# Cross-entropy backward on one core: loading two-row blocks as single transfers, and the last row in two column halves

## The chip, the cores and the metric

The kernel runs on one core of one Trainium2 chip. The metric is the device time of one execution in microseconds (us). The profile's span is 1.7 to 2.0 us shorter than the time of the same execution.

Some words that recur: HBM is the memory outside the core in which input and output lie. SBUF is the core's own memory, in 128 partitions. DMA engines, 16 of them here, copy between the two; loads and stores are issued on two separate DMA queues. VectorE and ScalarE are compute engines of the core. A "packet" is one entry of the profile's record of DMA work; here each packet of data moves one contiguous run of bytes.

## The reference

The input is 8192 rows of 8192 logits in float32 and one label per row. The output is the softmax of each row, with 1 subtracted at the label:

```python
logits_max = np.max(logits, axis=-1, keepdims=True)
exp_logits = np.exp(logits - logits_max)
softmax = exp_logits / np.sum(exp_logits, axis=-1, keepdims=True)
...
return (softmax - one_hot).astype(np.float32)
```

Every byte is read once and written once: 268.4 MB in and 268.4 MB out.

## The kernel before

A "row" of the program is 128 rows of the matrix, one on each SBUF partition, 4 MB (4096 KB) in all. There are T = 64 of them. A block is two neighbouring rows of the program, and in HBM the two lie side by side for each partition: partition p of a block has 2 x 32 KB in one run. SBUF holds six such rows ("slots"), and a row is worked on in place in its slot.

```python
SLOTS = 6
...
x_b = x_nv.rearrange("(b p j) v -> b p j v", p=P, j=G)      # G = 2 rows to a block
X = const.tile([P, SLOTS, V], fp32)
...
def load(t, n):
    free = [stored[u - SLOTS] for u in range(t, t + n) if u - SLOTS in stored]
    w = run(nc.sync, free, got[t % SLOTS], "dma_start", out=sbuf(t, n), in_=hbm(x_b, t, n))
    loaded.update(dict.fromkeys(range(t, t + n), w))

def store(t, n):
    w = run(nc.scalar, [finished[t + n - 1]], put[t % SLOTS], "dma_start", ...)
    stored.update(dict.fromkeys(range(t, t + n), w))
...
for t in range(T):
    # ScalarE: exp with accumulated sum; VectorE: reciprocal
    if t + 1 < T:
        load(t + 1, 1)
        row_max(t + 1)          # VectorE, waits for the load
    if t > 0:
        store(t - 1, 1)
    # ScalarE: scale by 1/sum; VectorE: subtract the one-hot
```

A load waits until the row six earlier has been stored, because it takes that row's slot. And on VectorE the maximum of row t + 1 stands ahead of the one-hot pass of row t, so row t can't be stored before row t + 1 has been loaded.

## Time and profile before

The time is 1248.08 us, the median of 3 runs (1248.03 to 1248.10). What matters of the profile:

| Quantity | Value | View |
|---|---|---|
| DMA engines, share of time busy | 1.00 in the middle | windows |
| Rate moved | 433 GB/s in the middle | windows |
| VectorE | 90% of the span | page, part 1 |
| ScalarE | 74% of the span | page, part 1 |
| One load, issue to landing | 24.2 us (median) | page, part 6 |
| One store, issue to landing | 55.1 us (median) | page, part 6 |

These are lines of the page of the kernel before. The first two are the busy tenths and the rate in 40 slices of the span. Then come the DMA queues (q1 is the loads', q10 the stores'; packets, MB, share of the engines), two groups of VectorE instructions, and the issues (count, KB each, us from issue to landing).

```profile
DMA  9999999999999999999999999999999999999998
GB/s 406 418 430 433 435 434 430 433 435 433 431 434 434 433 431 434 434 432 431 434 435 432 431 434 434 431 433 434 435 431 433 433 434 432 432 433 435 431 432 385
...
q1 hardware_dynamic: 9216, 268.44, 50.0%
q10 hardware_dynamic: 9264, 268.51, 49.9%
...
L64 DVE TENSOR_REDUCE m<-X 128x1 f32<-128x8192 f32 x64 | 555.6, 8681 | 91.4 <-DMA X<-in_logits_dram 91.4
...
X<-in_logits_dram SPq DMA_DIRECT2D x64, 4096.0 KB, 24.2
out_dram<-X ACTq DMA_DIRECT2D x64, 4096.0 KB, 55.1
```

The DMA engines are busy all the time and share themselves equally between loads and stores. VectorE waits 91.4 us in all for loads, about 2 us a row. Stores take long to land because they stand in a queue. With a row of 8.39 MB (in and out) every 19.36 us, the engines set the pace.

The windows view of the kernel before shows the start, the middle and the end. Its columns are the stretch, its length, the busy time of five engines (PE, PEld, DVE, ACT, POOL, with counts), the clock, the DMA share, and GB/s.

```profile
60.00:240.00 180.00, 0.00 (x0) 0.00 (x0) 180.00 (x33) 148.42 (x33) 0.00 (x0) 1.00 1.00 433
400.00:860.00 460.00, 0.00 (x0) 0.00 (x0) 413.34 (x73) 339.46 (x73) 0.00 (x0) 1.00 1.00 433
...
1224.00:1232.00 8.00, 0.00 (x0) 0.00 (x0) 5.57 (x2) 0.26 (x1) 0.00 (x0) 1.00 1.01 434
1232.00:1240.00 8.00, 0.00 (x0) 0.00 (x0) 0.00 (x0) 0.00 (x0) 0.00 (x0) 1.00 1.02 442
```

While the compute engines end their work at about 1230 us, stores are still queued, and the DMA engines stay full until about 1242 us.

The timeline of the kernel before shows when the last two rows arrive, and when the last store is issued (start, length, engine, what, and the idle time before it).

```profile
1179.83 8.69 DVE L64 TENSOR_REDUCE m<-X 128x1 f32<-128x8192 f32 x1 [1.92 <-DMA X<-in_logits_dram]
...
1199.19 8.69 DVE L64 TENSOR_REDUCE m<-X 128x1 f32<-128x8192 f32 x1 [1.94 <-DMA X<-in_logits_dram]
...
1229.60 0.34 ACTq L64 DMA_DIRECT2D out_dram<-X  x1
```

Both maxima start the moment their row has landed. The last row (63) lands 19.36 us after row 62, which is 4.19 MB at 217 GB/s, half of the 433.

### The profile page before, as it was taken

The page shows a single profiled execution, that of the slowest core. Times are in us where ns is not written, and L with a number is a line of the kernel's source. Part 1 is how long each engine was busy: PE and PEld are TensorE (multiplying, and loading weights), DVE is VectorE, ACT ScalarE, POOL GpSimd, SP SyncE. Part 2 cuts the span into 40 slices and gives each one's busy share as a digit, 9 for nine tenths or more (in the row PEclk, how much of TensorE's full clock was granted, in tenths as well). Part 3 has the DMA queues.
Part 4 walks back from the last instruction along what each step waited for, and adds up shares of the span by engine and source line. Part 5 has one row for each costly group of instructions (what it writes and reads, how often), then busy time and mean ns, then how long its engine had stood idle before and what let it go on. Part 6 is the DMA issues. An engine that isn't in the chain of part 4 may idle for free.

```text
span 1246.4 us, 592 instructions
## 1 busy us (share of the span) xinstructions
PE 0.4 (0%) x2; PEld 0.3 (0%) x2; DVE 1121.3 (90%) x196; ACT 919.0 (74%) x194; POOL 7.4 (1%) x7
## 2 busy tenths in 40 slices
PE   0000000000000000000000000000000000000000
PEld 0000000000000000000000000000000000000000
DVE  5999999999988989889898898998988989889893
ACT  3888888888767777677767777777777777677772
POOL 2000000000000000000000000000000000000000
DMA  9999999999999999999999999999999999999998
GB/s 406 418 430 433 435 434 430 433 435 433 431 434 434 433 431 434 434 432 431 434 435 432 431 434 434 431 433 434 435 431 433 433 434 432 432 433 435 431 432 385
DMA packets 18484, 536.98 MB, mean 431 GB/s; under 512 B 2064, under 2 KB 2064, under 8 KB 2096
## 3 DMA queue, kind: packets, MB, share of 16 engines
q1 hardware_dynamic: 9216, 268.44, 50.0%
q10 hardware_dynamic: 9264, 268.51, 49.9%
q14 instruction: 4, 0.03, 0.0%
HBM read 268.50 MB, written 268.44 MB: 431 GB/s over the span
## 4 chain that ended last, share of the span: by engine, by line
another core or an unknown queue 69%; DVE 21%; DMA 6%; SPq 1%; ACT 1%; DVEq 0%; issue 0%; PE 0%; ACTq 0%
DVE m L64 10%; DVE X L64 10%; DMA out_dram<-X 4%; DMA X<-in_logits_dram 2%; SPq L64 1%; ACT X L64 1%; DVE iota L64 0%; DVEq L52 0%; DMA lab_raw<-in_labels_dram 0%; DVE lab_f L64 0%; DVE r L64 0%; PE iota L64 0%; ACTq L64 0%; DVE lab L64 0%
## 5 line engine op out<-in xcount | busy, mean ns | idle before, releaser
L64 DVE TENSOR_REDUCE m<-X 128x1 f32<-128x8192 f32 x64 | 555.6, 8681 | 91.4 <-DMA X<-in_logits_dram 91.4
L64 ACT ACTIVATE X<-X,m 128x8192 f32<-128x8192 f32 x64 | 455.8, 7122 | 187.9 <-DVE m L64 187.9
L64 DVE SCALAR_TENSOR_TENSOR X<-iota,lab,X 128x8192 f32<-128x8192 int16 (+1 forms) x65 | 559.6, 8610 | 4.1 <-ACT X L64 4.1
L64 ACT ACTIVATE X<-X,r 128x8192 f32<-128x8192 f32 (+1 forms) x65 | 456.0, 7016 | 116.0 <-DVE r L64 116.0
L64 DVE RECIPROCAL r<-s 128x1 f32<-128x1 f32 x64 | 9.8, 153 | 7.3 <-ACT X L64 7.3
L64 ACT ACTIVATION_READ_ACCUMULATOR X<-X,m 128x1 f32 x64 | 11.9, 186 | 0.0
L64 DVE CAST lab_f<-lab_raw 32x256 f32<-32x256 int32 x1 | 3.5, 3526 | 4.9 <-DMA lab_raw<-in_labels_dram 4.9
L64 POOL IOTA X<- 128x8192 int16 x1 | 6.9, 6943 | 0.0
L64 DVE TENSOR_SCALAR iota<-X 128x4096 int32<-128x4096 int32 x1 | 4.4, 4427 | 0.1
L64 ACT ACT_TABLE_LOAD x1 | 1.3, 1283 | 1.4 <-SPq L52 1.4
L64 DVE COPY lab<-iota 128x64 f32<-128x64 f32 x1 | 0.2, 224 | 0.5 <-PE iota L64 0.5
L64 PE MATMUL iota<-ident,lab_f 32*128 32x32 f32 x2 | 0.4, 300 | 8.5 <-DVE lab_f L64 8.5
L64 PEld LDWEIGHTS iota<-ident,lab_f 32*128 32x128 f32 x2 | 0.3, 196 | 8.4 <-DVE lab_f L64 8.4
L64 POOL TENSOR_SCALAR_AFFINE_SELECT ident<-ident 32x32 f32<-32x32 f32 x1 | 0.2, 202 | 0.1
L64 POOL MEMSET ident<- 32x32 f32 x1 | 0.1, 114 | 0.5 <-SPq L52 0.5
L176 POOL MEMSET const-bfloat16-1.0<- 128x1 bf16 x1 | 0.1, 106 | 0.0
L176 POOL MEMSET const-uint8-127<- 128x1 uint8 x1 | 0.1, 106 | 0.0
L176 POOL MEMSET const-float32-0.0<- 128x1 f32 x1 | 0.1, 103 | 0.2 <-issue 0.2
L176 POOL MEMSET const-float32-1.0<- 128x1 f32 x1 | 0.1, 103 | 0.0
## 6 DMA issues: line engine op xcount, KB each, us to landing
X<-in_logits_dram SPq DMA_DIRECT2D x64, 4096.0 KB, 24.2
out_dram<-X ACTq DMA_DIRECT2D x64, 4096.0 KB, 55.1
lab_raw<-in_labels_dram ACTq DMA_DIRECT2D x1, 64.0 KB, 3.9
```

The lines of the kernel that those rows point to most:

```text
L64: instruction = getattr(engine, method)(**operands)
L176: nc = _bacc.Bacc("TRN2", target_bir_lowering=False, num_devices=1)
```

## The change

The intent is to give the DMA engines fewer and longer pieces of work. Blocks 4 to 25 (rows 8 to 51) are loaded as one transfer of 8 MB, whose runs are 64 KB long in HBM and in SBUF. The last row's load is cut into two column halves of 16 KB runs, so that its maximum can begin on the first half. Stores stay as they were: 4 MB, 32 KB runs. The core of the diff (cuts marked):

```diff
+PAIRED_LOADS = range(4, 26)
+PAIRED_STORES = ()
...
+        halves = [slice(0, V // 2), slice(V // 2, V)]
...
-        def load(t, n):
+        def load(t):
+            if t % G and t // G in PAIRED_LOADS:
+                return
+            n = G if t // G in PAIRED_LOADS else 1
             free = [stored[u - SLOTS] for u in range(t, t + n) if u - SLOTS in stored]
-            w = run(nc.sync, free, got[t % SLOTS], "dma_start", out=sbuf(t, n), in_=hbm(x_b, t, n))
+            to, of = sbuf(t, n), hbm(x_b, t, n)
+            cols = halves if t == T - 1 else [slice(None)]
+            w = [
+                run(nc.sync, free, got[q], "dma_start", out=to[:, :, c], in_=of[:, :, c])
+                for q, c in zip((t % SLOTS, SLOTS), cols)
+            ]
             loaded.update(dict.fromkeys(range(t, t + n), w))
...
         def row_max(t):
+            x, to = X[:, t % SLOTS, :], m[:, t : t + 1]
+            parts = [(x, to)] if len(loaded[t]) == 1 else [...]   # two halves, each into m_halves
...
+            if len(parts) == 2:
+                w = run(nc.vector, [w], dve, "tensor_tensor", out=to, ..., op=Alu.min)
```

More of the change, by code (lines that the diff above doesn't have):

```diff
@@ L47 @@
     m, s, r = (const.tile([P, T], fp32, name=n) for n in ("m", "s", "r"))
+    m_halves = const.tile([P, 2], fp32)
     iota = psum.tile([P, V], i16)
@@ L53 @@
         sem = tc.alloc_semaphore
-        got = [sem(f"got{i}") for i in range(SLOTS)]
+        got = [sem(f"got{i}") for i in range(SLOTS + 1)]
         put = [sem(f"put{i}") for i in range(SLOTS)]
@@ L107, in sbuf, with store @@
             return X[:, t % SLOTS : t % SLOTS + n, :]
-        def load(t, n):
+        def load(t):
+            if t % G and t // G in PAIRED_LOADS:
+                return
+            n = G if t // G in PAIRED_LOADS else 1
             free = [stored[u - SLOTS] for u in range(t, t + n) if u - SLOTS in stored]
-            w = run(nc.sync, free, got[t % SLOTS], "dma_start", out=sbuf(t, n), in_=hbm(x_b, t, n))
-            loaded.update(dict.fromkeys(range(t, t + n), w))
-        def store(t, n):
+            to, of = sbuf(t, n), hbm(x_b, t, n)
[4 more added lines that the diff above has]
+            ]
+            loaded.update(dict.fromkeys(range(t, t + n), w))
+        def store(t):
+            if t // G in PAIRED_STORES:
+                if t % G == 0:
+                    return
+                t -= t % G
+            n = G if t // G in PAIRED_STORES else 1
             w = run(
@@ L121, in row_max @@
         def row_max(t):
-            w_max.append(run(
-                nc.vector, [loaded[t]], dve, "tensor_reduce",
-                out=m[:, t : t + 1], in_=X[:, t % SLOTS, :], axis=mybir.AxisListType.X, op=Alu.max, negate=True,
-            ))
-        load(0, 1)
+            x, to = X[:, t % SLOTS, :], m[:, t : t + 1]
+            parts = [(x, to)] if len(loaded[t]) == 1 else [(x[:, c], m_halves[:, i : i + 1]) for i, c in enumerate(halves)]
+            for arrived, (part, extreme) in zip(loaded[t], parts):
+                w = run(
+                    nc.vector, [arrived], dve, "tensor_reduce",
+                    out=extreme, in_=part, axis=mybir.AxisListType.X, op=Alu.max, negate=True,
+                )
+            if len(parts) == 2:
+                w = run(
+                    nc.vector, [w], dve, "tensor_tensor",
+                    out=to, in0=m_halves[:, 0:1], in1=m_halves[:, 1:2], op=Alu.min,
+                )
+            w_max.append(w)
+        load(0)
         row_max(0)
@@ L137 @@
             if t + 1 < T:
-                load(t + 1, 1)
+                load(t + 1)
                 row_max(t + 1)
             if t > 0:
-                store(t - 1, 1)
-            n = 1 if t + 1 < T else 2
-            cols = [slice(i * V // n, (i + 1) * V // n) for i in range(n)]
+                store(t - 1)
+            cols = [slice(0, V)] if t + 1 < T else halves
             scaled = [
@@ L158 @@
             finished.append(w)
-        store(T - 1, 1)
+        store(T - 1)
         for w in dict.fromkeys(stored[t] for t in range(T - SLOTS, T)):
```

## The prediction

> **What bounds the kernel now.** The DMA engines. The page's slices show them 90% busy or more throughout, at 430 to 435 GB/s; windows over 500:600 and 600:700 us give a share of 1.00 at 434 and 433 GB/s. VectorE is second: 90% of the span, 17.3 us per row (maximum 8.68 us, one-hot pass 8.61 us, slightly overlapped), against a row period of 19.35 us (chain of waits). 8.39 MB in 19.35 us is 433.5 GB/s. The Trainium skill, "DMA: Bandwidth & Descriptors", section "Where 436 GB/s comes from", gives 435.2 GB/s as the ceiling of the 16 ports; the trace agrees, with no long stretch above it. So 536.9 MB cannot take less than 1233.6 us, and about 2 us of start and 3.5 us of end come on top (windows: next to nothing before 2 us, share 0.38 in 1242:1244, none after): floor about 1239 us of span against 1246.4. Better packets can win about 8 us.
>
> **What the change does.** 44 loads of 4 MB become 22 of 8 MB; bytes, VectorE and ScalarE work stay. If the missing 8 us is a cost per transfer (128 of them), each costs about 0.06 us; 22 fewer save about 1.4 us, all on the bound resource (an estimate from these numbers).
>
> Arbitration moves. The same page, section "Queues, rings and completion order", says an engine takes turns between queues packet by packet. This trace shows equal 32 KB packets and equal shares (50.0% and 49.9%). With 64 KB load packets I expect loads to get two thirds while a store is pending: an 8 MB load takes about 29 us plus 4 us latency, then stores run alone.
>
> Slots are freed in pairs. Three pairs circulate in three periods of 38.7 us = 116 us. From load issue to the second row's store landing I estimate 33 (load) + 56 (a period, then maximum and one-hot pass) + 14 (store) = 103 us, so some queue always remains and steady state stays DMA bound. At the entry (row 8) the pair waits for store 3 instead of store 2: the load issued at 108.8 us moves to about 116 us, and the DMA may run dry for 2 to 4 us once. At the end the last load goes in 16 KB packets against 32 KB store packets, so it may get only a third of the engines and land several us later; its split maximum wins 4.3 us back, and the last store has about 4 us slack (DMA busy to about 1243 us, last store issued at 1229.6 us, alone needs 9.7). Estimated cost 0 to 2 us.
>
> **Sum.** 1248.1 - 1.4 + 0 to 3: about 1247 us; 8 in 10 between 1242 and 1256. Chances: faster by over 2%: 0.01; within 2%: 0.95; slower by over 2%: 0.04.
>
> **What would show it.** 2,816 load packets of 64 KB, about 6,200 packets in the load queue instead of 9,216. DMA share still 1.00 at 433 to 435 GB/s in the middle; load landing 29 to 36 us for 8 MB; VectorE waiting for loads once per pair (about 4 us) rather than 2 us per row; a dip in the DMA share near 110:120 us; the last load landing late.
>
> **What would make it wrong.** Pairs starving the store queue so that the engines go dry every period (1% of DMA idle is 12 us); 64 KB packets moving slower, or being cut to 32 KB; a late last row that leaves the engines idle at the end.

## The result and the profile after

The kernel after takes 1250.63 us, the median of 6 runs (1249.83 to 1251.23), against 1248.07 us before (1247.91 to 1248.10, 6 runs). The ratio is 1.002 with a 95% interval of 1.0007 to 1.0033: the same within 2%, but slightly slower, clear of noise. Ratios here are the mean time of one kernel's runs over that of the other's of the same rounds, so not quite the ratio of the medians quoted.

These lines of the page of the kernel after answer to those shown of before.

```profile
DMA  9999999999999999999999999999999999999998
...
q10 hardware_dynamic: 9264, 268.51, 49.8%
q1 hardware_dynamic: 6192, 268.44, 49.8%
...
L68 DVE TENSOR_REDUCE m<-X 128x1 f32<-128x8192 f32 x63 | 546.5, 8675 | 92.5 <-DMA X<-in_logits_dram 92.5
...
out_dram<-X ACTq DMA_DIRECT2D x64, 4096.0 KB, 30.8
X<-in_logits_dram SPq DMA_DIRECT2D x19, 4096.0 KB, 27.4
X<-in_logits_dram SPq DMA_DIRECT2D x2, 2048.0 KB, 29.1
X<-in_logits_dram SPq DMA_DIRECT2D x22, 33.2
```

The load queue has 6,192 packets instead of 9,216: the 64 KB runs do go as one packet each. An 8 MB load lands in 33.2 us. If loads and stores still shared the engines equally, its 8.39 MB at 217 GB/s would take 38.7 us, so loads now get more than half while a store is pending. The trace's records of single packets show the turns directly: from 549 to 578 us, while such a load was on its way, 128 load packets of 64 KB and 128 store packets of 32 KB began, so the loads had two thirds of the bytes. Stores land sooner than before (30.8 instead of 55.1 us), because they stand in a shorter queue.

The chain of waits of the kernel after, over one turn of the ring of slots (start, length, what), is this:

```profile
469.68 32.91 DMA X<-in_logits_dram
...
502.61 8.69 DVE m L68
511.29 8.66 DVE X L68
...
519.98 27.04 DMA out_dram<-X
```

A pair is loaded, one maximum and the previous row's one-hot pass run, the store lands, and the next load but one is issued at 547.04 us: 77.4 us for two pairs. The kernel before takes as long. From the issue times of the loads, two rows took 38.72 us before (16 rows from 496.45 to 806.21 us) and 38.69 us after (10 pairs from 431.00 to 817.86 us).

The windows of the kernel after, as shown of before:

```profile
60.00:240.00 180.00, 0.00 (x0) 0.00 (x0) 168.41 (x30) 139.00 (x30) 0.00 (x0) 1.00 1.00 433
400.00:860.00 460.00, 0.00 (x0) 0.00 (x0) 413.37 (x73) 340.72 (x73) 0.00 (x0) 1.00 1.00 434
...
1224.00:1232.00 8.00, 0.00 (x0) 0.00 (x0) 4.80 (x2) 6.77 (x2) 0.00 (x0) 1.00 0.97 418
1232.00:1240.00 8.00, 0.00 (x0) 0.00 (x0) 4.08 (x1) 0.00 (x0) 0.00 (x0) 1.00 0.62 266
```

The rates of start and middle are as they were (VectorE now waits in the first stretch, busy 168 of 180 us instead of all of it, which costs nothing while the DMA engines are full). The end isn't: between 1232 and 1240 us the engines are busy for 62% only.

The timeline of the kernel after shows the last rows again.

```profile
1180.64 8.69 DVE L68 TENSOR_REDUCE m<-X 128x1 f32<-128x8192 f32 x1 [1.97 <-DMA X<-in_logits_dram]
...
1209.77 4.42 DVE L68 TENSOR_REDUCE m_halves<-X 128x1 f32<-128x4096 f32 x1 [7.39 <-DMA X<-in_logits_dram]
...
1236.11 0.34 ACTq L68 DMA_DIRECT2D out_dram<-X  x1
```

The second half of row 63 lands 29.1 us after row 62, not 19.4. That is 4.19 MB at 144 GB/s, a third of 433; from 1182 to 1208 us, 232 load packets of 16 KB and 228 store packets of 32 KB began. The last store is issued 6.5 us later than before (1236.11 against 1229.60 us), the queue of stores has run out before it, and the span ends with it, 12.3 us after its issue.

So the first theory is: the pairs are worth a few tenths of a microsecond, and the halved last load loses several at the end, because its 16 KB packets take turns with 32 KB packets. The first rival is that the pairs are what costs: slots come free in pairs, so the engines may run dry.

### The profile page after: what moved, and what is told of

Read it like the earlier page. It is cut to its first block, busy times and chain, and to the rows that moved or that the text cites. A ratio compares the mean times of both kernels' runs of the same rounds, so it can differ in the third digit from the quotient of the medians. Undisturbed runs are those within 1.5% of the kernel's fastest.

```text
span 1248.4 us, 595 instructions
## 1 busy us (share of the span) xinstructions
PE 0.4 (0%) x2; PEld 0.3 (0%) x2; DVE 1119.4 (90%) x198; ACT 919.0 (74%) x194; POOL 7.4 (1%) x7
## 3 DMA queue, kind: packets, MB, share of 16 engines
q1 hardware_dynamic: 6192, 268.44, 49.8%
## 4 chain that ended last, share of the span: by engine, by line
DMA 60%; DVE 38%; ACT 1%; DVEq 0%; issue 0%; PE 0%; SPq 0%; ACTq 0%
DMA X<-in_logits_dram 32%; DMA out_dram<-X 28%; DVE X L68 18%; DVE m L68 18%; ACT X L68 1%; DVE m_halves L68 0%; DVE iota L68 0%; DVEq L56 0%; DMA lab_raw<-in_labels_dram 0%; DVE lab_f L68 0%; DVE r L68 0%; PE iota L68 0%; SPq L68 0%; ACTq L68 0%; DVE lab L68 0%
## 5 line engine op out<-in xcount | busy, mean ns | idle before, releaser
L68 DVE TENSOR_REDUCE m<-X 128x1 f32<-128x8192 f32 x63 | 546.5, 8675 | 92.5 <-DMA X<-in_logits_dram 92.5
L68 DVE TENSOR_REDUCE m_halves<-X 128x1 f32<-128x4096 f32 x2 | 8.8, 4410 | 7.4 <-DMA X<-in_logits_dram 7.4
## 6 DMA issues: line engine op xcount, KB each, us to landing
out_dram<-X ACTq DMA_DIRECT2D x64, 4096.0 KB, 30.8
X<-in_logits_dram SPq DMA_DIRECT2D x2, 2048.0 KB, 29.1
X<-in_logits_dram SPq DMA_DIRECT2D x22, 33.2
```

The lines of the kernel that those rows point to most:

```text
L68: instruction = getattr(engine, method)(**operands)
```

## The experiments

All kernels gave correct results. Each was timed in five rounds beside the kernel before. Most means rest on 5 runs; those of the two kernels with padded pairs and of the paired stores rest on 4, those of the change and of the pairs as two loads on 6.

| Kernel | Median us | Ratio to before (95%) |
|---|---|---|
| the change | 1250.63 | 1.002 (1.0007 to 1.0033) |
| pairs, whole last load | 1247.67 | 0.9998 (0.9984 to 1.0011) |
| halved last load alone | 1249.33 | 1.001 (0.9998 to 1.0023) |
| halved last load and last stores | 1248.47 | 1.0003 (0.999 to 1.0015) |
| the change and halved last stores | 1247.58 | 0.9996 (0.9983 to 1.0009) |
| pairs from block 8 | 1248.16 | 1.0001 (0.9988 to 1.0014) |
| pairs, slots 64 B apart | 1270.44 | 1.0179 (1.0163 to 1.0194) |
| pairs, slots 256 B apart | 1267.91 | 1.0163 (1.0141 to 1.0184) |
| singles, slots 64 B apart | 1248.13 | 1.000 (0.9986 to 1.0013) |
| pairs as two loads | 1254.73 | 1.0059 (1.0045 to 1.0073) |
| pairs as two loads, stores halved | 1278.80 | 1.0247 (1.0233 to 1.0261) |
| loads and stores in pairs | 1338.24 | 1.072 (1.0705 to 1.0734) |

### Undoing the halved last load

```diff
-            cols = halves if t == T - 1 else [slice(None)]
+            cols = [slice(None)]
```

> The change without its halved last load (22 pairs kept). Theory: the change is two effects of opposite sign, the pairs save about 0.036 us for each transfer removed (0.8 us) and lose up to 1 us at the entry, the halves at the end cost about 3 us. So 1247.0 to 1248.0 us, the last load landing within 27 us of its issue, and the DMA share near 1.00 until 1240 us. Rival (the pairs are what costs, by engines going dry in the middle or at the entry): 1250 us or more, as with the whole change.

Measured: 1247.67 us (1247.46 to 1248.26). The pairs alone don't cost; the loss of the change is gone. The last load lands 26.7 us after its issue (1173.14 to 1199.85 us); the timeline at its landing and at the last store:

```profile
1199.85 8.69 DVE L68 TENSOR_REDUCE m<-X 128x1 f32<-128x8192 f32 x1 [1.96 <-DMA X<-in_logits_dram]
...
1230.26 0.34 ACTq L68 DMA_DIRECT2D out_dram<-X  x1
```

They save 0.44 us by the medians, and the interval of the ratio includes 1, so the size of the saving is not settled by this run. The rival falls.

### The halved last load alone

```diff
-PAIRED_LOADS = range(4, 26)
+PAIRED_LOADS = ()
```

> The kernel before with only the last load halved. Theory: the halves' 16 KB packets get a third of the engines beside 32 KB store packets, the second half lands 33 to 37 us after its issue rather than 24 us, the last store is issued about 6 us later (1236 rather than 1230 us) and the DMA is partly idle between 1220 and 1236 us: 1250 to 1252 us, that is 2 to 4 us over before. Rival (pairs cost): 1248 us, as before.

Measured: 1249.33 us (1249.28 to 1249.81), 1.2 us over before, less than expected; no single run overlaps with those of before (1248.00 to 1248.32). The timeline of this kernel (rows 62 and 63 landing, and the last store):

```profile
1179.95 8.69 DVE L68 TENSOR_REDUCE m<-X 128x1 f32<-128x8192 f32 x1 [1.94 <-DMA X<-in_logits_dram]
...
1208.98 4.42 DVE L68 TENSOR_REDUCE m_halves<-X 128x1 f32<-128x4096 f32 x1 [7.30 <-DMA X<-in_logits_dram]
...
1235.33 0.34 ACTq L68 DMA_DIRECT2D out_dram<-X  x1
```

Row 63 lands 29.0 us after row 62, again a third of the rate, with no pair anywhere in the kernel. The late end belongs to the halves.

### Giving the last stores packets of the same size

```diff
-            w = run(nc.scalar, [finished[t + n - 1]], put[t % SLOTS], "dma_start",
-                out=hbm(o_b, t, n), in_=sbuf(t, n))
+            for c in halves if 57 <= t <= 62 else [slice(None)]:
+                w = run(nc.scalar, [finished[t + n - 1]], put[t % SLOTS], "dma_start",
+                    out=hbm(o_b, t, n)[:, :, c], in_=sbuf(t, n)[:, :, c])
```

The edit was made to the halves alone, and later to the whole change.

> As the halves alone, and the stores of rows 57 to 62 also in two column halves, so that load and store packets are 16 KB both. If the share goes by packets in turn, the last load gets half of the engines again and lands 23 to 27 us after its issue, and the time is back at 1248 to 1249 us although two transfers and six stores were cut. Rival (cutting a load in two makes it late by itself, through a cost per transfer or the order within its own queue): landing 33 us or more, 1250 us or more.

Measured: 1248.47 us. In the timeline the second half of the last load lands 23.4 us after the pair of halves was issued (1177.52 us), against 33.9 us in the kernel with the halves alone (1175.05 to 1208.98 us):

```profile
1200.96 4.42 DVE L68 TENSOR_REDUCE m_halves<-X 128x1 f32<-128x4096 f32 x1 [2.54 <-DMA X<-in_logits_dram]
...
1228.53 0.34 ACTq L68 DMA_DIRECT2D out_dram<-X  x1
```

Nothing about the load was changed. Only the packets that it meets became smaller, and it got its half of the engines back. Cutting a load in two doesn't make it late by itself; the unequal sizes do.

> The whole change, and the stores of rows 57 to 62 in column halves, so that the last load meets packets of its own size. If the unequal packet sizes at the end are the whole cause of the change's loss, the second half of the last load lands 23 to 28 us after its issue rather than 36 us, the last store is issued before 1232 us, and the time falls from 1250.6 to 1247.5 to 1248.3 us. Rival (pairs and halves cost together in some other way): it stays above 1249.5 us.

Measured: 1247.58 us (1247.43 to 1247.88), 3.05 us under the change by the medians. Landing is again 23.4 us after the issue (1176.94 to 1200.36 us). The timeline:

```profile
1200.36 4.42 DVE L68 TENSOR_REDUCE m_halves<-X 128x1 f32<-128x4096 f32 x1 [1.89 <-DMA X<-in_logits_dram]
...
1227.92 0.34 ACTq L68 DMA_DIRECT2D out_dram<-X  x1
```

This is the whole change with nothing undone. The unequal packets at the end are the whole of its loss. The last store is issued 1.7 us earlier than in the kernel before, and still the gain is half a microsecond at most: its five runs all lie under the nine of the kernel before (1247.97 to 1248.32 us), but the interval of the ratio includes 1. At the end the engines are full either way (1.05 from 1232 to 1240 us, against 1.02 before), and the bytes decide.

### Where the pairs begin

```diff
-PAIRED_LOADS = range(4, 26)
+PAIRED_LOADS = range(8, 26)
```

(with a whole last load)

> Pairs in blocks 8 to 25 only, whole last load. The prediction had the engines run dry for 2 to 4 us where the pairs begin at row 8. If that were so, beginning at row 16 with more stores queued would give 1245 to 1246.5 us. The trace of the change shows no such gap (433 GB/s from 60 to 240 us), so I expect 1247.5 to 1248.1 us, the same as pairs from block 4 within 0.4 us.

Measured: 1248.16 us (1247.68 to 1248.57), by the medians 0.5 us over the pairs from block 4, just outside the 0.4 us that I had written, but with overlapping runs. There was no gap to remove.

### Cutting the pairs' packets to 32 KB

```diff
-    X = const.tile([P, SLOTS, V], fp32)
+    X = const.tile([P, SLOTS, V + 16], fp32, name="X")[:, :, :V]
```

(with a whole last load; V + 64 in the second version)

> Pairs with a whole last load, but the slots in SBUF stand 64 bytes apart, so that a pair's 64 KB run should be cut into two packets of 32 KB; still 22 transfers of 8 MB. If the share goes by packets, an 8 MB load lands after about 40 us rather than 33. If the saving of about 0.8 us goes with the packets it is gone (1248 to 1249 us); if it goes with the transfers it stays (within 0.3 us of the unpadded pairs). The load queue shows 6,176 packets with 64 KB runs and 8,992 if cut to 32 KB.

Measured: 1270.44 us. The shares behave as expected, and the time doesn't at all. The second version was to see whether odd start addresses were to blame, and a third run padded the kernel without pairs.

> Pairs of 2 x 32 KB packets again, with slots 256 bytes apart instead of 64. In the run with 64 bytes the engines were not idle (share 1.00) but moved 424 instead of 433 GB/s. If the odd start addresses of the slots made the packets slow, this run is back at 433 GB/s and at about 1248 us, with an 8 MB load landing after about 40 us (equal shares). If cutting the pair's run in two does it, whatever the address, it stays near 424 GB/s and 1265 to 1273 us.

> The kernel before (single loads, whole last load) with slots 64 bytes apart. If the odd start addresses make packets slow, 1260 us or more at 425 GB/s or less. If they are harmless, 1248 us at 433 GB/s, as before, and the slow packets of the padded pairs come from the cut pair.

Measured: 1267.91 us for pairs with slots 256 bytes apart, and 1248.13 us for single loads with slots 64 bytes apart. The addresses are harmless. The page (issues) and the windows of the pairs with 256 bytes:

```profile
X<-in_logits_dram SPq DMA_DIRECT2D x22, 8192.0 KB, 39.2
...
400.00:860.00 460.00, 0.00 (x0) 0.00 (x0) 406.44 (x71) 333.31 (x70) 0.00 (x0) 1.00 1.00 425
```

The load queue had 8,864 packets, 2,816 more than with unpadded pairs (6,048), so each 64 KB run was cut in two. (The 8,992 and 6,176 that I had written were miscounts.) An 8 MB load now lands in 39.2 us instead of 33: equal packets, equal shares. But the engines moved 425 GB/s at a share of 1.00. The trace's records of single packets show how both can be true: from 400 to 860 us, most 32 KB packets (92% of the loads', 98% of the stores') took 1213 ns, as before, but some took up to 2149 ns in the load queue and 2401 ns in the store queue, and the means were 1247 and 1222 ns. An engine that is stuck in a packet counts as busy. The sum of the excess, 3047 load packets by 34 ns and 2926 store packets by 9 ns over 16 engines, is 8.1 us of 460, or 1.8%, which is the missing rate. The rest of the 20 us is such packets outside this stretch and a late end: row 63 landed at 1224.37 us, and from 1232 to 1256 us the engines were busy for about 70%. What makes these packets long isn't settled. The trace shows when they come: from 180 to 1000 us, 12.6 of 13.6 us of this excess lay in packets that began within 5 us of the issue of a load or store (37% of the packets). In the kernel before, all the excess in this stretch is 0.1 us.

### Pairs freed together, but loaded row by row

```diff
-            w = [run(nc.sync, free, got[q], "dma_start", out=to[:, :, c], in_=of[:, :, c])
-                for q, c in zip((t % SLOTS, SLOTS), cols)]
-            loaded.update(dict.fromkeys(range(t, t + n), w))
+            for u in range(n):
+                w = run(nc.sync, free, got[(t + u) % SLOTS], "dma_start", out=to[:, u, :], in_=of[:, u, :])
+                loaded[t + u] = [w]
```

> Blocks 4 to 25 loaded as before, row by row in transfers of 4 MB and 32 KB packets, but both issued only when both slots are free, as a pair is; whole last load. It separates the two parts of the padded pairs, which lost 20 us. If the late freeing of slots with equal shares is their cause, this too runs at 425 to 429 GB/s in the middle and 1260 us or more. If it is the order of the packets in an 8 MB transfer (two packets of one partition one after the other), this is back at 433 GB/s and 1248 to 1250 us.

Measured: 1254.73 us (1253.34 to 1260.30), between the two expectations. The run that was profiled is the slowest of the six, so its late end is probably larger than that of the median run. The windows view of this kernel, and its timeline where row 63 lands:

```profile
400.00:860.00 460.00, 0.00 (x0) 0.00 (x0) 414.25 (x71) 338.97 (x72) 0.00 (x0) 1.00 1.00 433
...
1224.00:1232.00 8.00, 0.00 (x0) 0.00 (x0) 8.00 (x2) 7.21 (x2) 0.00 (x0) 1.00 0.07 29
...
1215.76 8.69 DVE L68 TENSOR_REDUCE m<-X 128x1 f32<-128x8192 f32 x1 [1.95 <-DMA X<-in_logits_dram]
```

The middle is at 433 GB/s, so late freeing of slots doesn't make packets slow. Its price is elsewhere. The engines were as busy as before, yet the last row lands 16.6 us later (1215.76 against 1199.19 us): over the whole run the stores have been served ahead of the loads (when row 63 had landed, 12.8 MB were left to store, against 19.4 MB before). Then nothing is queued while the last rows are computed, and the engines idle (7% busy from 1224 to 1232 us). With 64 KB packets this doesn't happen: with pairs and a whole last load, row 63 landed at 1199.85 us.

### Restoring the ratio of sizes with smaller stores

From this I formed a further theory: 64 KB packets make up for the late freeing only because they are twice the size of the stores' packets.

```diff
+            for c in halves if t // G in PAIRED_LOADS else [slice(None)]:
+                ...   # the store of rows 8 to 51 in two column halves, added to the last kernel
```

> The kernel that issues each pair as two 4 MB loads of 32 KB packets (1254.7 us), now with the stores of blocks 4 to 25 cut into two column halves of 16 KB packets. The load packets are then again twice the size of the store packets, as in the change, with no packet of 64 KB. If the change's 64 KB packets helped only by giving the loads two thirds of the engines, which makes up for the late freeing of slots, the last load no longer lands late (row 63 ready near 1200 us rather than 1216 us) and the time is back at 1248 to 1250 us, the 44 more store transfers costing up to 1.8 us. Rival (64 KB runs help by themselves): still 1254 us or more.

Measured: 1278.80 us (1276.05 to 1280.62). The theory failed its test. The chain of waits and the windows:

```profile
478.01 20.88 DMA X<-in_logits_dram
...
516.66 43.31 DMA out_dram<-X
...
400.00:860.00 460.00, 0.00 (x0) 0.00 (x0) 395.72 (x70) 329.06 (x70) 0.00 (x0) 1.00 1.00 422
```

The shares did shift: the first load of a pair lands after 20.9 us instead of 26.6 us. But long packets appeared here too (means of 1246 ns for the 32 KB loads and 622 for the 16 KB stores, whose usual durations are 1213 and 611), the rate fell to 422 GB/s, and row 63 landed at 1230.96 us. Whether the ratio alone would have sufficed at 433 GB/s stays open, and so does the cause of the long packets.

### Stores in pairs too

```diff
-PAIRED_STORES = ()
+PAIRED_STORES = range(4, 26)
```

(with a whole last load)

> Loads and stores of blocks 4 to 25 both in pairs with 64 KB packets, whole last load. If the share goes by packets it is equal again, an 8 MB load beside a store lands after 38 to 43 us. If the saving is about 0.036 us per transfer removed and the queues never run dry, 44 fewer transfers give 1246.3 to 1247.0 us. Rival: the store of a first row now waits for its partner, so the engines run dry in each period: a share below 0.99 in the middle and 1252 us or more.

Measured: 1338.24 us, far slower than even the rival had it. The chain of waits over one turn of the ring, and the windows:

```profile
411.03 37.64 DMA X<-in_logits_dram
...
448.69 8.69 DVE m L68
457.38 8.66 DVE X L68
...
466.07 29.96 DMA out_dram<-X
...
400.00:860.00 460.00, 0.00 (x0) 0.00 (x0) 379.75 (x66) 316.12 (x67) 0.00 (x0) 1.00 0.96 395
```

The first row of a block waits for the second before both are stored. Load, compute and store of a pair then follow each other in 85.0 us for two pairs (411.03 to 496.05 us) where the engines need 77.4, and both queues are sometimes empty: a share of 0.96. Beside it, the load packets were long (a mean of 2663 instead of 2418 ns). That is as large a part of the loss: 1376 load packets by 245 ns over 16 engines are 21.1 us of 460, or 4.6%, beside 4% of idle time. Here nearly all of the excess (36.5 of 36.8 us from 180 to 1000 us) lay in packets that began within 5 us of an issue, 22% of all. The 38 to 43 us that I expected for a load beside a store don't settle the shares: loads took 37.6 and about 28 us in turn, as every second one ran nearly without a store beside it.

## Why the prediction was right or wrong

The time (1247 predicted, 1250.63 measured) lies inside the range, and "the same" was right. Its terms fared differently.

- **What bounds the kernel: right.** Share 1.00 at 433 GB/s before, and 434 after. This is also why 22 fewer transfers bought almost nothing: there was little to buy. The Trainium skill, "DMA: Bandwidth & Descriptors", section "Where 436 GB/s comes from", has 435.2 GB/s as the ceiling of the 16 SBUF ports, and no run here moved more than 434 from 400 to 860 us. The lower limit of about 358 that the section has for transfers from and to HBM was not met: here 433 held over 460 us.
- **Packets and shares: right.** Exactly 2,816 runs of 64 KB went as packets, and 8 MB landed in 33.2 us (29 + 4 predicted). The section "Queues, rings and completion order" of the same page says that an engine takes turns between queues packet by packet; these runs agree for three ratios: 16 to 32 KB gave a third (4 MB in 29.1 us), equal sizes gave half (19.4 us), and 64 to 32 KB gave two thirds (128 packets of each from 549 to 578 us).
- **The saving, "22 fewer save about 1.4 us": too large.** The trace has 1213 ns for a 32 KB packet and 2418 ns for a 64 KB one, so joining two saves 8 ns, and 8 packets per engine and a completion packet of 9 ns make 73 ns a pair, or 1.6 us: about the estimate. But the period of two rows fell by only 0.03 us (38.72 to 38.69), about 0.7 us for 22 pairs, and the time of the pairs alone by 0.44 us. Between the two kernels with halved last stores, without and with pairs, the medians fell by 0.89 us (1248.47 to 1247.58), with no overlapping runs. Some 64 KB packets were longer (mean 2421 ns), which gives back 8 x 2.6 = 21 ns a pair; and packets of two queues overlap a little in the records, so that not each of their nanoseconds is time. The 8 us that I had put down to transfers rested on a floor of 1233.6 us, an estimate from the 435.2 GB/s named above. Most of them lie inside the packets: 32 KB in 1213 ns on 16 engines is 432 GB/s.
- **The steady state, "103 us of 116, so some queue always remains": right in its outcome, not in its sum.** No dry engines in the middle, and VectorE waits for a load once a pair (25 waits, 92.5 us in all). But the turn took all of the 116 us: the load issued at 431.00 us landed after 33.4, the store of its second row was issued 55.6 later, and landed after 27.0 instead of 14, just when the next load into these slots was issued (547.04 us). Loads had no slack; what kept the engines full was the queue of stores.
- **The entry, "the DMA may run dry for 2 to 4 us once": wrong.** The load moved even further than I had it, from 108.80 to 120.89 us. But from 60 to 240 us the engines moved 433 GB/s as before, and beginning the pairs later didn't help (1248.16 us). I had worked out when one store would drain, and taken its landing for the moment at which the queue was empty; the stores behind it covered the gap.
- **The end, "estimated cost 0 to 2 us": the mechanism was right, the term mis-sized.** The last load got a third of the engines and came late, as predicted. In the profiled runs the terms add up: row 63 landed 10.6 us later than in the kernel before, the split maximum took 4.1 of it back (the last store is issued 6.5 us later), and the store had 4.5 us of slack, as the span ended 16.8 us after its issue before and ends 12.3 us after it now. That leaves 2.0 us, the difference of the spans (1248.4 and 1246.4), with what the pairs saved already in it. By the medians, what the halves cost is 1.2 us with the halves alone and 3.05 us within the change. I had added up a saving and a cost as if they were independent, and they aren't. In the kernel before, the bytes set the end, so a saved nanosecond of DMA counts. With halves, the last row's chain sets the end: the last store runs alone, and the span ends 12.3 us after its issue in the change (1236.11 to 1248.4 us) and as long after it with the halves alone (1235.33 to 1247.7 us). Then saved DMA time counts for nothing. Worse, with pairs row 62 landed 0.69 us later (1180.64 against 1179.95 us), and the end moves with it. This nearly covers the 0.76 us between the two profiled runs (1250.22 and 1249.46), and 0.7 of the 1.3 us between the two medians. The rest is open: the runs of the change scatter by 1.4 us, those of the halves alone by 0.5.

The cost at the end can be seen in the bytes as well. From 1216 to 1240 us the kernel before moves 434, 434 and 442 GB/s in three windows of 8 us, the change 422, 418 and 266: a deficit of 1.63 MB, or 3.8 us at 433 GB/s. The end is only 2.0 us later, because the change was 0.16 MB ahead at 1216 us, and because the kernel before drains its last bytes slowly: 1.15 MB in the 4.8 us after 1240 us, where the change needs 6.9 us for 2.62 MB.

The experiments left two kernels at the level of the one before, pairs with a whole last load (1247.67 us) and the change with halved last stores (1247.58 us). Both beat the change; neither beats the kernel before by more than its interval.

## What to carry to other kernels

Where loads and stores share busy DMA engines, the run length of a transfer sets not only its overhead but its share against the other queue: here a load in 16 KB packets beside stores in 32 KB packets got a third of the engines and came 10 us late. Before cutting the last transfer so that compute can begin sooner, look whether the end is set by queued bytes or by the last row's chain; if it's the bytes, there is nothing to win and the chain can become the new limit. And add up the terms of an estimate only as long as they act on the same bound: a saving on the old limit is worth nothing once the change has made another one.

## What the Trainium skill lacked or had wrong

- "DMA: Bandwidth & Descriptors", "Queues, rings and completion order": it describes a packet as some 9 to 17 descriptors and doesn't say what that means for shares. Here, as the shares show, the turn was one contiguous run: two queues shared the engines by the ratio of their run lengths (16 to 32 KB: 29.1 us for 4 MB; equal: 19.4 us), and a transfer of 8 MB cut into runs of 32 KB landed in 39.2 us instead of 33, although its transfer was still twice the store's.
- The same page, "Rules for kernel authors", advises to coalesce many small transfers into one large one. It lacks how little is left to gain above that once both queues are full (from 4 to 8 MB, two rows in 38.69 instead of 38.72 us), and that coarser transfers can cost far more than they save: with six slots, stores in pairs too took 1338 us.
- No page has the long packets: at a busy share of 1.00 the engines moved 425 GB/s where 8 MB loads were cut into 32 KB runs, and 422 GB/s with stores cut into halves, against 433, because some packets took up to twice their usual 1213 ns or more. Most of the excess came within 5 us of an issue where loads were cut (12.6 of 13.6 us) and with paired stores (36.5 of 36.8 us), less clearly with halved stores (8.4 of 15.0 us). A share of 1.00 alone doesn't show that the engines are at their ceiling. The cause is open.
- "HBM Reference", "Specifications (TRN2)": it has a core that streams alone at about 425 GB/s; here the kernel before held 433 GB/s over 460 us, loads and stores together.
